# A Fox/RWKV-7 block on one core: q and k stored once per pair of heads, and the order of vector work in the RWKV stage

## The chip, the core and the metric

The kernel runs on one NeuronCore of a Trainium2 chip. The metric is the device time of one execution in microseconds (us). The engines are named as the profile names them: PE (TensorE, matmuls; PEld is its weight load), DVE (VectorE, elementwise work), ACT (ScalarE, activations), POOL (GpSimd), SP (SyncE, which here only issues DMAs; SPq is its queue).

## What is computed

One transformer block over 1,024 tokens of width 1,024, in float32: a norm modulated by a condition c, one wide projection `w_in`, two branches that mix over time, a gate for each branch, an output projection, a second modulated norm, and a convolutional feed-forward net. The two branches matter here. The first is causal attention with forget gates (8 heads of 64); the second is the RWKV-7 recurrence (8 heads of 64):

```python
logits = einsum('bhqd,bhkd->bhqk', q, k) * scale + cum[:, :, q0:q1, None] - cum[:, :, None, :q1]
probs = softmax(where(causal, logits, -inf)); o = einsum('bhqk,bhkd->bhqd', probs, v)

def step(state, inp):
    r_t, w_t, k_t, v_t, a_t, b_t = inp
    sa = einsum('bhvk,bhk->bhv', state, a_t)
    state = state * w_t[..., None, :] + sa[..., None] * b_t[..., None, :] + v_t[..., None] * k_t[..., None, :]
    return state, einsum('bhvk,bhk->bhv', state, r_t)
```

## The kernel before, in words

**Precision.** Most products are made of three passes: each operand is split into a rounded high part (hi, made on ACT) and the rest (lo, made on DVE), and hi·hi, hi·lo and lo·hi are added up in PSUM. One projection tile of 128 columns and 512 tokens is 24 matmuls. The split of a loaded weight tile is `load_w` (L272: hi on L288, lo on L290).

**Stages.** Projections of the low-rank parts and their chain (to about 145 us of the span), the RWKV stage (to about 611 us), attention (to about 820 us), then the branch outputs, `w_o` and the feed-forward net, which the change doesn't touch.

**How work is woven.** PE's instructions run in the order of the program (`manual_schedule`). The program is written by a small planner, `Weave` (L49): chains of dependent work are Python generators that yield a number of nanoseconds; until that much matmul time has been given out, the planner fills PE with steps of queued projections (L105, L117). `weave.now` is the planner's own clock; it counts matmuls only. The chains have ranks: main before pre. The queue of fillers holds q and k of the attention heads (`qk_steps`, L406, eight weight tiles), v (`v_steps`, L963, two) and sixteen gate tiles (`gate_steps`, L343; in attention `late_gate`, L1174, where the bank is named rk_ps). The r, k, v tiles of RWKV go ahead of these. The order of the other engines in the RWKV stage is not the program's: a scheduler with a timeline of its own sets it from readiness and program order, and `add_manual_dep` with NOSYNC puts one instruction of an engine behind another one of the same engine.

**q and k.** For each pair of heads (i % 4) and each half of the tokens `qk_steps` makes qh on ACT (L413) and ql on DVE (L415), both in a ring of two buffers (sp0), and stores them to DRAM tensor `d_st` (L419). `d_st` has four planes for each head: [q hi; q lo], [k hi; k hi], [q hi; forget rows], [k lo; forget rows]. So some parts are stored twice, with two DMAs each of 64 rows: six DMAs of 128 KB for one half. `forget` (L644) stores the four rows of the forget gates for all heads (L684, L685). `load_head` (L1017) loads a head for attention with three DMAs from POOL: stA (planes 0 and 1, 128 rows), stB (planes 2 and 3, 68 rows), vh.

**A unit of RWKV** is one pair of heads and one half of the tokens (eight chunks of 64); there are eight units, k = 0 to 7. `pre` (L720) makes a unit's operands:

- cum, el, en (decays), the norm of kk by a head sum (ssq), then eight elementwise steps on DVE: ar (L760), kr (L761), bk (L762), ar (L764), al (L765, L766), bk (L767), rkb (L771), given out together; then `yield 10500`;
- p, the products of a chunk (L784), masked into E on DVE (L787);
- the inverse of the triangular 32x32 blocks: E's blocks go through DRAM (sm, L795) to the tile M (M32 in the code, L799), then 31 steps of two DVE instructions (L807, L809), back through DRAM (se, L812) to TT (L820);
- q, a product whose copy to QA is L846, and the bonus (bon, L850), made from the head sum bs. The scan of cum (L737) of the next unit is placed behind the bonus.

`main` (L853) continues once `ready` is reached, a time on the planner's clock set at L800 (E's end plus 49,500, 38,500 or 41,000): X on DVE (two transposes, L865), placed behind marks such as the last state (S) and the last E; xi, zi, uw, mz and the chain of states (sp, yp); then y, its mean by a head sum (mu), y minus mean on DVE (L946), the square, its head sum (va), and the end of the norm. A head sum (`head_sums`, L710) makes hi on ACT (L712) and lo on POOL (L715), yields 3,400 and issues two matmuls.

**After the RWKV stage** the first head's loads are given out (L1027), the gate in hand is completed (L1031), and attention begins; its logits (`s_chain`, L1047) wait 10,500 ns of filling gate matmuls.

Of the kernel before, what the change touches and what calls it, by code (L numbers as in the profile page):

```python
# [10 lines left out]
F32R = mybir.dt.float32r  # L11
AF = mybir.ActivationFunctionType
ALU = mybir.AluOpType
# [3 lines left out]
S = 1024  # L17
# [5 lines left out]
CH = 64  # L23
# [12 lines left out]
NOSYNC = mybir.DependencyInfo(mybir.DependencyClass.NoSync, mybir.DependencyReason.DATA)  # L36
# [96 lines left out]
def hybrid_block(ctx: ExitStack, tc: tile.TileContext, a, out):  # L133
    nc = tc.nc
    weave = Weave()
# [23 lines left out]
    dr = ctx.enter_context(tc.tile_pool(name="dr", bufs=1, space=bass.MemoryType.DRAM))  # L159
# [6 lines left out]
    def V(name, i=0, n=1):  # L166
        o, _ = VEC[name]
        return vec[:, o + i : o + i + n]
# [30 lines left out]


    d_gate = dr.tile([16, 128, S], F32, name="d_gate")
    d_st = dr.tile([8, 4, 128, S], F32R, name="d_st")
    d_v = dr.tile([8, 128, 8, 128], F32R, name="d_v")
    d_orw = dr.tile([4, 128, S], F32, name="d_orw")

# [34 lines left out]
            nc.vector.tensor_tensor(dst[:, cs], ps, bb[:, cs], op=ALU.add)  # L240

    marks = {}
    held = []

    def behind(i, x):
# [120 lines left out]
    with ExitStack() as es:  # L366
# [39 lines left out]
        def qk_steps(w, i):  # L406
            sc_ = 0.125 if i < 4 else 1.0
            for hf in range(2):
                cs = slice(hf * NH, hf * NH + NH)
                ps = big(f"qk{i}_{hf}")  # L410
                yield from gemm_steps(ps, w, u, cs)
                hi = gsp.tile([128, NH], F32R, tag="sp0", name=f"qh{i}_{hf}")
                nc.scalar.activation(hi, ps, AF.Copy, scale=sc_)  # L413
                lo = gsp.tile([128, NH], F32R, tag="sp0", name=f"ql{i}_{hf}")
                stt(lo, ps, sc_, f32(hi), op0=ALU.mult, op1=ALU.subtract)  # L415
                h0 = 2 * (i % 4)
                for t, k, r0 in ((hi, 0, 0), (lo, 0, 64), (hi, 2, 0)) if i < 4 else ((hi, 1, 0), (hi, 1, 64), (lo, 3, 0)):
                    for h in range(2):
                        nc.sync.dma_start(f32(d_st[h0 + h, k, r0 : r0 + 64, cs]), f32(t[h * 64 : h * 64 + 64, :]))  # L419

        HS = (slice(0, 64), slice(64, 128))

# [10 lines left out]
        with tc.tile_pool(name="st", bufs=1) as st, tc.tile_pool(name="stp", bufs=2, space=PS) as stp, \  # L433
# [144 lines left out]
        with tc.tile_pool(name="lg", bufs=1, reuse_waits="tile") as lg, \  # L578
# [65 lines left out]
            def forget():  # L644
# [10 lines left out]
                for hf in range(2):  # L655
                    cs = slice(hf * NH, hf * NH + NH)
                    ps = gen(f"f_{hf}")
                    n = 0
                    for x in u:
                        for kt in range(KT):  # L660
# [20 lines left out]
                    nc.scalar.copy(r[:, 3, :], z)  # L681
                    nc.scalar.activation(r[:, 4, :], f32(r[:, 0, :]), AF.Copy, scale=-1.0)
                    nc.scalar.activation(r[:, 5, :], f32(r[:, 1, :]), AF.Copy, scale=-1.0)
                    nc.sync.dma_start(f32(d_st[:, 2, 64:68, cs]), f32(r[:, 0:4, :]))  # L684
                    nc.sync.dma_start(f32(d_st[:, 3, 64:68, cs]), f32(r[:, 2:6, :]))  # L685

            for p in range(4):
                for i in (p, 4 + p):
# [6 lines left out]
        def c3(ap):  # L695
            return ap.rearrange("p (c s) -> p c s", s=CH)
# [23 lines left out]
        def pre(k, p, hf):  # L720

            n = f"{p}_{hf}"
            cs = slice(hf * NH, hf * NH + NH)
# [5 lines left out]
            def chunk_tile(nm, bufs, *dims):  # L729
                return rw.tile([128, *dims], F32, tag=nm, name=f"{nm}{n}", bufs=bufs)  # L730
# [5 lines left out]
            for c0 in (0, 256):  # L736
                i = nc.vector.tensor_tensor_scan(cum[:, c0 : c0 + 256], cst2[:, 128:384], cum[:, c0 : c0 + 256], initial=0.0,  # L737
                                                 op0=ALU.mult, op1=ALU.add)
# [19 lines left out]
                yield 200  # L758
            ar = chunk_tile("ar", 2, 2, NCU, CH)
            stt(ar[:, 0], c3(kr), nkk[:, p : p + 1], el[:, :, 0:CH], op0=ALU.mult, op1=ALU.mult)  # L760
            stt(kr, kr, V("k_k", p), al, op0=ALU.mult, op1=ALU.mult)  # L761
            tt(bk[:, :, 0, :], c3(kr), c3(en), op=ALU.mult)  # L762
            nc.gpsimd.tensor_copy(bk[64:128, :, 2, :], bk[64:128, :, 0, :])
            tt(ar[:, 1], c3(rr), el[:, :, 1:], op=ALU.mult)  # L764
            ts(al, al, V("k_a", p), oka[:, p : p + 1], op0=ALU.mult, op1=ALU.add)  # L765
            tt(al, al, kk, op=ALU.mult)  # L766
            tt(bk[:, :, 1, :], c3(al), c3(en), op=ALU.mult)  # L767
            pcd = chunk_tile("pcd", 3, NCU)
            nc.gpsimd.tensor_copy(pcd, el[:, :, CH])
            rkb = tmp("ksq")  # L770
            stt(rkb, rr, V("r_k", p), al, op0=ALU.mult, op1=ALU.mult)  # L771
            yield 10500


            while (k - 2, 0) not in passed:
# [1 line left out]
            E = chunk_tile("E", 2, NCU, 2, 3, CH)  # L777
# [19 lines left out]
            M32 = chunk_tile("M32", 1, 32, 32)  # L797
            for g in range(4):
                nc.sync.dma_start(M32[g * 32 : g * 32 + 32, :, :], sm.rearrange("h c b s t -> (h c b) s t"))  # L799
            ready = weave.now + (49500 if k == 0 else 38500 if k < 5 else 41000)  # L800
            E32 = chunk_tile("E32", 1, 8, 32)
            nc.gpsimd.dma_start(E32, a["cst"][:, CST["einit"][0] :].rearrange("p (j t) -> p j t", t=32))
            t32 = tmp("t32", 128)
            for s in range(31):
                J, W = s // 4 + 1, 31 - s
                tv = t32[:, 0 : J * W].rearrange("p (j w) -> p j w", w=W)
                tt(tv, E32[:, 0:J, s : s + 1].to_broadcast([128, J, W]),  # L807
                   M32[:, s : s + 1, s + 1 : 32].to_broadcast([128, J, W]), op=ALU.mult)
# [37 lines left out]
            nc.vector.tensor_copy(QA[:, :, 0, :], c3(q))  # L846
# [3 lines left out]
            marks["bonus"] = tt(bon, bp, vv, op=ALU.mult)  # L850
            units[p, hf] = dict(ready=ready, pcd=pcd, ar=ar, E=E, QA=QA, TT=TT, bon=bon, UV=UV)

        def main(k, p, hf):  # L853
# [9 lines left out]
            yield max(0, o["ready"] - weave.now - 2500)  # L863
            for h in range(2):
                i = nc.vector.transpose(X[B0[h], :, :], TT[B0[h], :, 0:32])  # L865
# [80 lines left out]
            stt(y, mu, -1.0 / CH, y, op0=ALU.mult, op1=ALU.add)  # L946
# [68 lines left out]
    heads = {}  # L1015

    def load_head(h):  # L1017
        A = at.tile([128, 2, S], F32R, tag="stA", name=f"stA{h}")
        nc.gpsimd.dma_start(A, d_st[h, 0:2, :, :].rearrange("k r s -> r k s"))
        B = at.tile([128, 2, S], F32R, tag="stB", name=f"stB{h}")  # L1020
        nc.gpsimd.dma_start(B[0:68, :, :], d_st[h, 2:4, 0:68, :].rearrange("k r s -> r k s"))
# [1050 lines left out]
```

## Time and profile before

| what | value |
|---|---|
| median of three runs | 1649.46 us (1647.59 to 1650.44) |
| the profiled execution | 1648.58 us |
| its span, first to last instruction | 1646.8 us |
| mean granted clock of PE | 0.994 |
| busy: PE, DVE, ACT, POOL | 1606.6, 1214.0, 827.6, 159.2 us |

The durations below come from that one profiled execution, and times within it count from the start of its span. A row of a timeline has the start and the duration in us, the engine, the line, the operation, output and inputs, shapes, and in brackets the idle time of the engine ahead of it and what ended this. A row of waits reads: who waited, for whom, us in total, times, the longest. A row of stretches (such as "190.00:192.00") has the length, the busy time and the number of instructions of PE, PEld, DVE, ACT and POOL, then PE's granted clock, the share of the DMA engines and GB/s. Names have no buffer numbers: E32 is E, M32 is M, t32 is t.

### The profile page before, as it was taken

Reading aid. Unit: us, or ns where it says so; the run is one execution under the profiler, and the core shown is the slowest. Engines: PE = TensorE matmul, PEld = TensorE weight load, DVE = VectorE, ACT = ScalarE, POOL = GpSimd, SP = SyncE. Lnnn points to the kernel's source line nnn. Section 1 sums busy time; section 2 is a strip of 40 time slices with the busy share of each in tenths; the row PEclk is TensorE's granted clock in tenths of the full one; section 3 lists DMA queues with packets and bytes.
Section 4 is the critical chain, followed back from the end, with each engine's and each line's share of the span. In section 5 each row is a group of like instructions: output and inputs, shape, how many; then the busy total and the mean of one; then the engine's idle time right before and its main releaser. Section 6 shows DMA issues by size and latency. Waiting matters only on the chain.

```text
span 1646.8 us, 25966 instructions
## 1 busy us (share of the span) xinstructions
PE 1606.6 (98%) x9694; PEld 1339.6 (81%) x9694; DVE 1214.0 (74%) x2345; ACT 827.6 (50%) x1557; POOL 159.2 (10%) x189
## 2 busy tenths in 40 slices
PE   7999999999999999999999999999999999999998
PEld 7777788898978788888888888788888888888886
DVE  4786787878876536888678547887777777886677
ACT  5563345444445656777623235644444444555455
POOL 0011101111111011333132000000000000000000
PEclk9999999999999999999999999999999999999999
DMA  9397645543433336434197420242232232675363
GB/s 338 121 344 229 183 130 139 137 117 94 114 103 98 97 122 163 128 106 118 50 357 264 175 80 26 84 135 96 96 120 98 96 109 96 223 256 160 122 211 109
DMA packets 121646, 240.60 MB, mean 146 GB/s; under 512 B 40048, under 2 KB 48880, under 8 KB 121520
## 3 DMA queue, kind: packets, MB, share of 16 engines
q1 hardware_dynamic: 113040, 220.58, 41.2%
q0 software_dynamic: 8480, 18.37, 4.2%
q8 instruction: 76, 1.25, 0.3%
q14 instruction: 50, 0.41, 0.1%
HBM read 173.35 MB, written 65.54 MB: 145 GB/s over the span
## 4 chain that ended last, share of the span: by engine, by line
PE 58%; DVE 5%; ACT 2%; DMA 2%; issue 1%; SPq 0%; POOL 0%; ACTq 0%; DVEq 0%; POOLq 0%
PE X L141 13%; PE D L141 13%; PE Y L141 6%; PE wo L141 5%; PE br L141 5%; PE W L141 3%; PE rk_ps L141 3%; PE gt L141 3%; PE ov L141 2%; PE lg L141 2%; PE tp L145 1%; DMA vh<-d_v 1%; DVE quads L1075 1%; DVE P L1085 1%; DVE tl L1115 0%
## 5 line engine op out<-in xcount | busy, mean ns | idle before, releaser
L141 PE MATMUL D<-op,op 128*128 128x512 f32 x924 | 209.8, 389 | 0.0
L141 PEld LDWEIGHTS D<-op,op 128*128 128x128 f32 x924 | 173.3, 188 | 36.3 <-DVE op L1295 0.3
L141 PE MATMUL X<-T_m,S 128*128 128x512 f32 x440 | 107.8, 390 | 1.7 <-ACT T_m L1756 1.1
L141 PEld LDWEIGHTS X<-T_m,S 128*128 128x128 f32 x440 | 82.4, 188 | 20.4 <-ACT T_m L1756 2.5
L1294 ACT CAST op<-g 128x512 fp32r<-128x512 f32 x77 | 47.8, 621 | 72.9 <-PE D L141 47.6
L1295 DVE TENSOR_TENSOR op<-g,op 128x512 fp32r<-128x512 f32 x77 | 53.0, 689 | 41.2 <-ACT op L1294 41.2
L1553 DVE SCALAR_TENSOR_TENSOR c<-ab,vec,c 128x512 f32<-128x512 f32 x88 | 65.9, 750 | 18.4 <-ACT c L1556 16.8
L807 DVE TENSOR_TENSOR t<-E,M 128x60 f32<-128x60 f32 (+24 forms) x248 | 55.7, 224 | 26.7 <-DMA M<-sm 20.7
L1519 DVE TENSOR_TENSOR A<-ur,A 128x512 fp32r<-128x512 f32 x64 | 44.0, 689 | 38.7 <-ACT A L1515 38.5
L1519 DVE TENSOR_TENSOR S<-ur,S 128x512 fp32r<-128x512 f32 x66 | 45.5, 691 | 35.2 <-ACT S L1515 35.0
L1515 ACT CAST S<-ur 128x512 fp32r<-128x512 f32 x66 | 41.0, 622 | 55.8 <-DVE ur L1508 30.6
L290 DVE TENSOR_TENSOR lo_in<-raw_in,hi_in 128x512 fp32r<-128x512 f32 x84 | 55.5, 701 | 15.3 <-PE gt L141 4.5
L141 PE MATMUL Y<-T_h,A 128*128 128x512 f32 x264 | 63.7, 390 | 0.3 <-ACT T_h L1756 0.3
L288 ACT CAST hi_in<-raw_in 128x1024 fp32r<-128x1024 f32 x42 | 43.9, 1050 | 40.0 <-PE qk L141 18.6
L141 PE MATMUL Y<-T_h,S 128*128 128x512 f32 x264 | 63.5, 390 | 0.4 <-ACT T_h L1774 0.4
L809 DVE TENSOR_TENSOR E<-E,t 128x60 f32<-128x60 f32 (+24 forms) x248 | 57.6, 232 | 6.3
L1115 DVE TENSOR_TENSOR tl<-tp,th 128x512 fp32r<-128x512 f32 (+1 forms) x80 | 50.0, 631 | 15.3 <-ACT th L1112 15.1
L1515 ACT CAST A<-ur 128x512 fp32r<-128x512 f32 x64 | 39.6, 621 | 42.9 <-PE X L141 31.3
L141 PE MATMUL W<-B_f,A 128*128 128x512 f32 x252 | 60.6, 389 | 0.0
L141 PE MATMUL X<-B_b,A 128*128 128x512 f32 x252 | 60.5, 389 | 0.0
L141 PEld LDWEIGHTS Y<-T_h,S 128*128 128x128 f32 x264 | 49.5, 188 | 11.0 <-ACT T_h L1774 0.8
L141 PEld LDWEIGHTS Y<-T_h,A 128*128 128x128 f32 x264 | 49.5, 188 | 11.0 <-ACT T_h L1756 0.7
(485 smaller groups left out, 4160.6 us busy)
## 6 DMA issues: line engine op xcount, KB each, us to landing
raw_in<-in_w_in SPq DMA_DIRECT2D x50, 512.0 KB, 3.7
wm<-in_w_mod SPq DMA_DIRECT2D x48, 512.0 KB, 7.4
ur<-in_w_up SPq DMA_DIRECT2D x44, 512.0 KB, 4.0
g<-d_g SPq DMA_DIRECT2D x35, 512.0 KB, 4.1
d_g<-gs SPq DMA_DIRECT2D x44, 256.0 KB, 2.1
d_g<-c SPq DMA_DIRECT2D x33, 256.0 KB, 4.5
d_st<-qh SPq DMA_DIRECT2D x64, 128.0 KB, 2.5
stA<-d_st POOLq DMA_DIRECT2D x8, 1024.0 KB, 8.1
```

What stands on the lines that cost most here:

```text
L141: nc.tensor.matmul(o, lhsT, rhs, start=start, stop=stop, skip_group_check=more)
L145: nc.tensor.transpose(o, i, eye)
L288: nc.scalar.copy(hi, raw)
L290: nc.vector.tensor_tensor(lo[:, c : c + NH], raw[:, c : c + NH], f32(hi[:, c : c + NH]), op=ALU.subtract)
L807: tt(tv, E32[:, 0:J, s : s + 1].to_broadcast([128, J, W]), M32[:, s : s + 1, s + 1 : 32].to_broadcast([128, J, W]), op=ALU.mult)
L809: tt(E32[:, 0:J, s + 1 : 32], E32[:, 0:J, s + 1 : 32], tv, op=ALU.add)
L1115: tt(tl[:, 0:w], tp[:, 0:w], f32(th[:, 0:w]), op=ALU.subtract)
L1294: nc.scalar.copy(hi, src)
L1295: tt(lo, src, f32(hi), op=ALU.subtract)
L1515: nc.scalar.copy(hi, src)
L1519: tt(lo, src, f32(hi), op=ALU.subtract)
L1553: stt(c, ab[:, x + hf * NH : x + hf * NH + NH], V("conv_w", 22 * x + i), c, op0=ALU.mult, op1=ALU.add)
```

## The change

Five edits:

1. **q and k once per pair.** `d_st` is replaced by `d_qk` (for each pair of heads: q hi, q lo, k hi, k lo, 128 rows each) and `d_f` (the forget rows for each head). `qk_steps` issues two DMAs of 128 rows for a half. `load_head` puts stA and stB together from five loads on POOL, with vh: stA's rows 0 to 63 (planes 0 and 2), its rows 64 to 127 (planes 1 and 2), stB's rows 0 to 63 (planes 0 and 3), stB's four forget rows, vh.
2. **First inverse step.** In unit 0 the first of the 62 inverse instructions is placed on DVE behind q's copy and behind the bonus.
3. **First main chain later.** The ready time of unit 0 goes from 49,500 to 51,500 ns.
4. **Steps singly.** Seven yields of 800 ns stand between the elementwise steps of every unit, and the yield behind them goes from 10,500 to 4,900.
5. **Last X behind y.** In units 5 to 7 X is placed behind the y minus mean (L946) of the unit before.

```diff
-    d_st = dr.tile([8, 4, 128, S], F32R, name="d_st")
+    d_qk = dr.tile([4, 4, 128, S], F32R, name="d_qk")
+    d_f = dr.tile([8, 2, 4, S], F32R, name="d_f")
...
+    first_step = []
+
+    def after_this(i):
+        for x in first_step:
+            tc.add_manual_dep(x.ins, i.ins.name, NOSYNC)
...
-                h0 = 2 * (i % 4)
-                for t, k, r0 in ((hi, 0, 0), (lo, 0, 64), (hi, 2, 0)) if i < 4 else ((hi, 1, 0), (hi, 1, 64), (lo, 3, 0)):
-                    for h in range(2):
-                        nc.sync.dma_start(f32(d_st[h0 + h, k, r0 : r0 + 64, cs]), f32(t[h * 64 : h * 64 + 64, :]))
+                for t, x in ((hi, 0), (lo, 1)) if i < 4 else ((hi, 2), (lo, 3)):
+                    nc.sync.dma_start(f32(d_qk[i % 4, x, :, cs]), f32(t))
...
-                    nc.sync.dma_start(f32(d_st[:, 2, 64:68, cs]), f32(r[:, 0:4, :]))
-                    nc.sync.dma_start(f32(d_st[:, 3, 64:68, cs]), f32(r[:, 2:6, :]))
+                    nc.sync.dma_start(f32(d_f[:, 0, :, cs]), f32(r[:, 0:4, :]))
+                    nc.sync.dma_start(f32(d_f[:, 1, :, cs]), f32(r[:, 2:6, :]))
...
             stt(ar[:, 0], c3(kr), nkk[:, p : p + 1], el[:, :, 0:CH], op0=ALU.mult, op1=ALU.mult)
+            yield 800
             stt(kr, kr, V("k_k", p), al, op0=ALU.mult, op1=ALU.mult)
+            yield 800
...
-            yield 10500
+            yield 4900
...
-            ready = weave.now + (49500 if k == 0 else 38500 if k < 5 else 41000)
+            ready = weave.now + (51500 if k == 0 else 38500 if k < 5 else 41000)
...
-                tt(tv, E32[:, 0:J, s : s + 1].to_broadcast([128, J, W]),
-                   M32[:, s : s + 1, s + 1 : 32].to_broadcast([128, J, W]), op=ALU.mult)
+                i = tt(tv, E32[:, 0:J, s : s + 1].to_broadcast([128, J, W]),
+                       M32[:, s : s + 1, s + 1 : 32].to_broadcast([128, J, W]), op=ALU.mult)
+                if k == 0 and s == 0:
+                    first_step.append(i)
...
-            nc.vector.tensor_copy(QA[:, :, 0, :], c3(q))
+            after_this(nc.vector.tensor_copy(QA[:, :, 0, :], c3(q)))
...
             marks["bonus"] = tt(bon, bp, vv, op=ALU.mult)
+            after_this(marks["bonus"])
+            first_step.clear()
...
-                for x in ("S", "E", "bank") if k == 0 else ("S", "E", "QA") if k > 4 else ("S", "E"):
+                for x in ("S", "E", "bank") if k == 0 else ("S", "E", "QA", "y") if k > 4 else ("S", "E"):
...
-            stt(y, mu, -1.0 / CH, y, op0=ALU.mult, op1=ALU.add)
+            marks["y"] = stt(y, mu, -1.0 / CH, y, op0=ALU.mult, op1=ALU.add)
...
-        nc.gpsimd.dma_start(A, d_st[h, 0:2, :, :].rearrange("k r s -> r k s"))
+        nc.gpsimd.dma_start(A[0:64, :, :], rows[:, 0:3:2, :])
+        nc.gpsimd.dma_start(A[64:128, :, :], rows[:, 1:3, :])
...
-        nc.gpsimd.dma_start(B[0:68, :, :], d_st[h, 2:4, 0:68, :].rearrange("k r s -> r k s"))
+        nc.gpsimd.dma_start(B[0:64, :, :], rows[:, 0:4:3, :])
+        nc.gpsimd.dma_start(B[64:68, :, :], d_f[h].rearrange("k r s -> r k s"))
```

More of the change, by code (lines that the diff above doesn't have):

```diff
@@ L760, in pre @@
             stt(ar[:, 0], c3(kr), nkk[:, p : p + 1], el[:, :, 0:CH], op0=ALU.mult, op1=ALU.mult)
+            yield 800
             stt(kr, kr, V("k_k", p), al, op0=ALU.mult, op1=ALU.mult)
+            yield 800
             tt(bk[:, :, 0, :], c3(kr), c3(en), op=ALU.mult)
             nc.gpsimd.tensor_copy(bk[64:128, :, 2, :], bk[64:128, :, 0, :])
+            yield 800
             tt(ar[:, 1], c3(rr), el[:, :, 1:], op=ALU.mult)
+            yield 800
             ts(al, al, V("k_a", p), oka[:, p : p + 1], op0=ALU.mult, op1=ALU.add)
+            yield 800
             tt(al, al, kk, op=ALU.mult)
+            yield 800
             tt(bk[:, :, 1, :], c3(al), c3(en), op=ALU.mult)
+            yield 800
             pcd = chunk_tile("pcd", 3, NCU)
@@ L1017, in load_head @@
     def load_head(h):
+        rows = d_qk[h // 2, :, h % 2 * 64 : h % 2 * 64 + 64, :].rearrange("k r s -> r k s")
         A = at.tile([128, 2, S], F32R, tag="stA", name=f"stA{h}")
-        nc.gpsimd.dma_start(A, d_st[h, 0:2, :, :].rearrange("k r s -> r k s"))
+        nc.gpsimd.dma_start(A[0:64, :, :], rows[:, 0:3:2, :])
+        nc.gpsimd.dma_start(A[64:128, :, :], rows[:, 1:3, :])
         B = at.tile([128, 2, S], F32R, tag="stB", name=f"stB{h}")
-        nc.gpsimd.dma_start(B[0:68, :, :], d_st[h, 2:4, 0:68, :].rearrange("k r s -> r k s"))
+        nc.gpsimd.dma_start(B[0:64, :, :], rows[:, 0:4:3, :])
+        nc.gpsimd.dma_start(B[64:68, :, :], d_f[h].rearrange("k r s -> r k s"))
         vh = at.tile([128, 8, 128], F32R, tag="vh", name=f"vh{h}")
```

## The prediction

> **What bounds the kernel now.** I read the page first, then the waits of the matmul engine over the stretch that the change touches (100 to 640 us), then the timelines around each wait.
>
> ```profile
> span 1646.8 us, 25966 instructions
> PE 1606.6 (98%) x9694; PEld 1339.6 (81%) x9694; DVE 1214.0 (74%) x2345; ACT 827.6 (50%) x1557; POOL 159.2 (10%) x189
> ```
>
> The matmul engine (PE) is busy for 1606.6 of 1646.8 us, and the change leaves every matmul as it is. So time can come only from the 40.2 us in which PE stands, and from a lower clock; and time can be lost only by new waits of PE. The waits of PE from 100 to 640 us are few (columns: us in total, times, longest):
>
> ```profile
> PE qk L141 <- DVE ql L415: 1.9, 1, 1.9
> PE v L141 <- DVE vs L978: 1.4, 2, 0.9
> PE rk_ps L141 <- ACT gm L1197: 1.4, 2, 1.2
> PE sp L141 <- ACT S L926: 1.0, 1, 1.0
> PE va L141 <- ACT Zts L712: 1.0, 1, 1.0
> PE va L141 <- POOL Wts L715: 0.9, 1, 0.9
> PE f L141 <- ACT z L619: 0.8, 1, 0.8
> PE zi L141 <- ACT X L875: 0.8, 1, 0.8
> PE p L141 <- DVE bk L767: 0.4, 1, 0.4
> PE mu L141 <- POOL Wtr L715: 0.4, 1, 0.4
> ```
>
> Together they are 10.0 us. So no version of this change can win more than about 10 us and the clock that a stall costs.
>
> **The first inverse step behind q's copy.** VectorE (DVE) around the longest wait:
>
> ```profile
> 182.96 0.19 DVE L807 TENSOR_TENSOR t<-E,M 128x31 f32<-128x31 f32 x1 [6.58 <-DMA M<-sm]
> ...
> 183.30 0.69 DVE L846 COPY QA<-q 128x512 f32<-128x512 f32 x1
> ...
> 186.85 0.68 DVE L850 TENSOR_TENSOR bon<-bs,v 128x512 f32<-128x512 f32 x1
> 187.45 1.26 DVE L737 TENSOR_TENSOR_SCAN cum<-cst,cum 128x256 f32<-128x256 f32 x2
> ...
> 189.94 0.69 DVE L415 SCALAR_TENSOR_TENSOR ql<-qk,qh 128x512 fp32r<-128x512 f32 x1
> ```
>
> The first inverse step of unit 0 stands at the head of DVE's queue for 6.58 us, waiting for M. Behind it stand q's copy, the bonus, the scan of the next unit and the split L415 (ql) that frees the bank PE wants. The inputs of the first two are there early:
>
> ```profile
> 176.49 1.15 PE L141 MATMUL q<-UV,E 64*64 64x64 f32 x32
> ...
> 181.55 0.39 PE L141 MATMUL bs<-al,blk_r 128*128 128x512 f32 x1
> ```
>
> So q's copy can run at 177.7 and the bonus at 182.0, both inside the 6.58 us, and M lands at 182.96 anyway: the first step loses nothing by the new order. Were bs late, the 62 steps behind the first, the store of E, TT, X and unit 0's xi would be late with it, which the later main chain covers up to its 2 us. Of the crowd ahead of ql, 0.60 + 0.60 us go (start to next start, as bon to cum). The scan, 1.18 us from start to start, is held behind the bonus only, so it can go too. PE's stall is 1.87 (the 1.9 above): 0.67 of it stays if the scan doesn't move, none if it does. I take 0.3. The stall also costs clock:
>
> ```profile
> 190.00:192.00 2.00, 1.32 (x5) 1.09 (x6) 1.93 (x7) 1.59 (x3) 0.07 (x1) 0.89 0.12 30
> 192.00:194.00 2.00, 2.00 (x7) 1.51 (x6) 1.79 (x8) 0.00 (x0) 0.00 (x0) 0.50 0.86 190
> 194.00:196.00 2.00, 2.00 (x8) 1.64 (x7) 2.00 (x6) 0.00 (x0) 0.12 (x1) 0.76 0.97 359
> ```
>
> The third number from the right is the granted clock: 2 x (0.11 + 0.50 + 0.24) = 1.7 us of matmul time lost. A gap that is split doesn't do that:
>
> ```profile
> 464.00:467.00 3.00, 1.13 (x4) 0.60 (x4) 0.40 (x1) 2.90 (x6) 1.26 (x1) 1.00 0.66 175
> ```
>
> Here PE stood for 1.02 and then 0.85 us at clock 1.00. So a rest of 0.3 should cost no clock. **Term 1: -(1.6 + 1.7) = -3.3 us**; bounds 0 (the order of DVE comes out with ql late all the same) and -3.6. [...]
>
> **The last X behind y.** Unit 5's X stands ahead of unit 4's y:
>
> ```profile
> 456.60 0.39 PE L141 MATMUL mu<-Wtr,blk_r 128*128 128x512 f32 x1
> ```
>
> ```profile
> 461.70 0.43 DVE L865 STREAM_TRANSPOSE X<-TT 32x256 f32<-32x256 f32 x1 [3.63 <-DMA TT<-se]
> 462.17 0.69 DVE L946 SCALAR_TENSOR_TENSOR y<-mu,y 128x512 f32<-128x512 f32 x1
> ```
>
> Its input mu is done at 457.0, and y starts at 462.17; from y hang the square, its split on ACT and POOL, and the va matmuls that wait 1.02 and 0.85 us. With y first it runs in the 3.63 us of idle, and X is delayed at most by its 0.69, and only if TT lands in that moment. **Term 2: -1.9 us**, bounds 0 and -2.6 (zi's 0.8 behind it might go too).
>
> **The steps given out singly.** In the old order all eight steps of a unit come at one place of the program, and the v evacuations behind them stand in their queue:
>
> ```profile
> 342.08 0.37 ACT L977 CAST vs<-v 128x256 fp32r<-128x256 f32 x1 [2.86 <-PE v L141]
> ```
>
> ```profile
> 345.14 0.42 DVE L978 TENSOR_TENSOR vs<-v,vs 128x256 fp32r<-128x256 f32 x1
> ```
>
> The ACT half of this evacuation ended at 342.45, the DVE half starts 2.7 us later; PE waits for it here and in one more place, 1.4 us together. Seven yields of 800 put later evacuations between the steps (GpSimd's copies of bk and pcd move along, off PE's path): **term 3: -1.4 us**, bounds 0 and -1.4. The steps themselves come up to 5.6 us later of 10.5 (the last yield shrinks from 10,500 to 4,900, so p keeps its place). PE waits for a unit's steps in one unit of eight (p, 0.4), so most units have slack; one evacuation of 0.6 to 0.7 us put ahead costs a unit without slack that much. **Term 4: +0.5 us**, bounds 0 and +1.4 (two units).
>
> **q and k stored once per pair.** Sixty-four of 96 DMA issues leave SyncE (each half had six of 128 KB; now two of 256 KB), and 12 MB written become 8. The buffers of qh and ql come free earlier; one such wait lay in the middle of unit 0's steps, ahead of the p matmul that waited 0.4 us:
>
> ```profile
> 158.59 0.69 DVE L415 SCALAR_TENSOR_TENSOR ql<-qk,qh 128x512 fp32r<-128x512 f32 x1 [1.99 <-DMA d_st<-ql]
> ```
>
> **Term 5: -0.4 us**, bounds 0 and -0.4. On the other side GpSimd issues five loads per head, not three: q/k in three parts of 64 rows (512 KB each), 4 rows of f (32 KB), vh.
>
> ```profile
> stA<-d_st POOLq DMA_DIRECT2D x8, 1024.0 KB, 8.1
> stB<-d_st POOLq DMA_DIRECT2D x8, 544.0 KB, 13.5
> vh<-d_v POOLq DMA_DIRECT2D x8, 512.0 KB, 3.9
> ```
>
> The 68-row stB is the slowest to land, though half of stA. A 512 KB part lies between vh's 3.9 and stB's 13.5 us; I take a value near vh and stA, 4 to 8. Head 0 is the tight one:
>
> ```profile
> 608.90 1.00 POOL L1021 DMA_DIRECT2D stB<-d_st  x1
> ```
>
> ```profile
> stB<-d_st POOLq DMA_DIRECT2D x1, 544.0 KB, 18.9
> ```
>
> ```profile
> 628.24 0.40 PE L141 MATMUL lg<-stB 68*128 68x512 f32 x1
> ```
>
> Its stB landed 18.9 us after 608.90, at 627.8, and the first matmul on it ran at 628.24. At stB's 1.00 us an issue, the third q/k part is issued 1.3 us later than stB was. **Term 6: 0**; its cover is the 10.5 us of gate matmuls given out ahead of the first logits and the rest of the gate before. Bounds 0 and +4.6 (below). The later heads are loaded while most of a head is still computed.
>
> **First main chain later.** 2,000 ns more of filling matmuls before unit 0's X and all that follows. It is no work and no wait: PE does projections in that time, and the two DMAs of a unit's end (gg in, d_orw out) move with it on SyncE's queue. **0**. Some of the shift is swallowed before the last unit, whose start hangs on its own ready time:
>
> ```profile
> 560.53 0.46 PE va L141 x2
> ...
> 567.12 0.62 PE xi L141 x32
> ```
>
> There are 6.1 us from the end of unit 6's va to unit 7's xi, where the code needs 1.3.
>
> **The sum.** -3.3 - 1.9 - 1.4 + 0.5 - 0.4 = -6.5 us. All engines but PE are ordered by a planner that counts with its own durations, and the new waits and edges reorder them. The waits of PE that the change doesn't aim at (sp, zi, mu, f: 3.0 us) show what an order leaves over; I add 0.8 for new ones: **-5.7 us**. The profiled execution took 1648.58 (1646.8 and 1.8 around it) and lies 0.88 under the median, 1649.46: 1642.9 by the one, **1643.8** by the other, which I forecast.
>
> **The rivals.**
>
> 1. A new DVE crowd, or ql late as before: one gap of the kind seen, 1.87 + 1.7, eats 3.6 of the gain: 1647.4. For it: DVE is 74% busy and 62 inverse steps fill its queue. Against: the gap needed a queue blocked for 6.58 us first. Chance 0.14; two such gaps (1651) 0.04.
> 2. The dip of the clock isn't the stall's, and stays: term 1 is -1.6, 1645.5. For it: at 464 to 467 as much idle time, in two pieces, left the clock at 1.00. Against it: the dip begins in the very slice in which the gap of 1.87 ends. Chance 0.05.
> 3. The half loads are as slow as stB was: the last of them lands 18.9 us after an issue 1.3 us later than stB's, at 629.1, and the shift of the chain can leave up to 2 us less of the gate before, so the logits want it at 626.2: 2.9 us of stall and 1.7 of clock, +4.6: 1648.4. [...] Chance 0.04.
> 4. **Slower**: the chain of unit 7 ends past a gate's boundary.
>
> ```profile
> 611.34 1.99 PE L141 MATMUL gt<-u_hi,hi_in 128*128 128x512 f32 x8
> ...
> 616.79 1.98 PE L141 MATMUL rk_ps<-u_hi,hi_in 128*128 128x512 f32 x8
> ```
>
> After the last va the program completes the gate in hand: 24 matmuls, 5.45 us, until 616.79. If va moves back by more than these 5.45 us, a tenth gate (48 matmuls, 10.9 us) is begun and completed there, and attention has six of the sixteen gates to fill its waits instead of seven:
>
> ```profile
> L141 PE MATMUL gt<-u_hi,lo_in 128*128 128x512 f32 x144 | 39.6, 400 | 0.0
> ```
>
> These are nine gates of 16. If attention can't do without the seventh, that is +10.9: 1654.7. Against: the shift is 2.0 us at most and 1.6 of overshoot (seven yields, a matmul of 0.23 each). Chance 0.07.
>
> **Chances and range.** Forecast case 0.60; all waits of the stage gone as well (-10 and less, about 1639) 0.06; rivals 0.14, 0.04, 0.05, 0.04, 0.07. A measurement of this kernel tells some 0.2% (3.3 us) from no change. Faster by more (under 1646.2): 0.60 + 0.06 + 0.05 = 0.71; within: 0.18; slower: 0.11. The range, 1639.0 to 1650.0, takes in rivals 1 to 3 and leaves out some of the best case, rival 4 and the double of rival 1.
>
> **What would show it.** After the change the waits of PE should lack qk <- ql near 190, va <- Zts and Wts near 465, and v <- vs; the granted clock should stay 1.00 from 180 to 200; QA and bon should stand ahead of the first t<-E,M; stB's landing should fall from 13.5 to under 8 us; nine gates should still end before the first rk_ps. Wrong would be: a new wait of over 1.5 us with a slice under clock 0.9, a wait of lg on a load, or gt with 160 instead of 144 matmuls of each kind.

## The result, and the profile after

After the change the median is 1679.69 us (1675.95 to 1680.91, five runs), beside 1647.59 us of the kernel before on the same chip: ratio 1.0189, 95% interval 1.0177 to 1.0200. The change makes the kernel slower by 1.9%. The profiled execution took 1675.95 us, with a span of 1674.2; before it was 1646.8. So there are 27.4 us to account for (this execution was the fastest of the five; by the medians it is 32). The page of the kernel after:

```profile
span 1674.2 us, 25916 instructions
PE 1616.7 (97%) x9694; PEld 1345.3 (80%) x9694; DVE 1218.8 (73%) x2345; ACT 828.0 (49%) x1555; POOL 160.9 (10%) x203
```

PE has the same 9,694 matmuls, is busy 10.1 us longer (the granted clock, 0.991 over the span after 0.994, is at most 5.4 us of it) and stands 57.5 instead of 40.2 us. Where, shows a table of stretches from 100 us on, cut at the first rk_ps (the start of attention) and at the first branch output. Before:

```profile
100.00:616.79 516.79, 507.95 (x4418) 420.08 (x4418) 375.59 (x980) 250.79 (x464) 73.77 (x98) 1.00 0.48 141
616.79:819.88 203.09, 195.34 (x1201) 169.76 (x1200) 155.13 (x302) 148.06 (x337) 55.47 (x68) 1.00 0.40 110
819.88:1646.80 826.92, 816.31 (x3637) 674.20 (x3636) 616.16 (x951) 375.57 (x673) 24.23 (x15) 1.00 0.43 146
```

After:

```profile
100.00:651.52 551.52, 532.74 (x4503) 439.21 (x4502) 384.59 (x987) 259.45 (x479) 78.57 (x104) 0.99 0.42 127
651.52:845.83 194.31, 180.22 (x1105) 156.51 (x1104) 149.16 (x294) 137.79 (x317) 55.16 (x75) 0.98 0.46 104
845.83:1674.20 828.37, 817.63 (x3637) 675.41 (x3636) 617.20 (x951) 375.55 (x673) 22.29 (x15) 0.99 0.43 146
```

The RWKV stage is 34.7 us longer and attention 8.8 us shorter. That is not yet the loss, because gates have moved from the one into the other (groups of the kernel after: count, busy us, mean ns):

```profile
L141 PE MATMUL gt<-u_hi,lo_in 128*128 128x512 f32 x176 | 47.2, 399 | 0.0
L141 PE MATMUL rk_ps<-u_hi,lo_in 128*128 128x512 f32 x80 | 23.7, 406 | 0.0
```

176 matmuls of a kind are eleven gates, not nine; attention has five, not seven. Two gates are 21.8 us of PE (twice the 10.9 of the prediction). Without them the RWKV stage lost 34.7 - 21.8 = 12.9 us. Attention should have become 21.8 shorter and became 8.8 shorter: 13.0 lost. PE stands 14.1 instead of 7.8 us in it, at a granted clock of 0.98. The rest of the kernel lost 1.4.

The order on PE shows why. Before, first product of the third pair's r, k, v, and the first norm (ssq) that needs them:

```profile
295.75 1.09 PE L141 MATMUL ps_rkv<-u_hi,hi_in 128*128 128x512 f32 x4
...
328.29 0.63 PE L141 MATMUL ssq<-kp,blk_r 128*128 128x512 f32 x2
```

After, with the end of the stage:

```profile
292.74 1.11 PE L141 MATMUL v<-hi_v,u_hi 128*128 128x256 f32 x8
...
328.10 0.39 PE L141 MATMUL ps_rkv<-u_hi,hi_in 128*128 128x512 f32 x1
...
358.72 0.63 PE L141 MATMUL ssq<-kp,blk_r 128*128 128x512 f32 x2
...
598.38 0.69 PE L141 MATMUL xi<-X,E 32*32 32x32 f32 x32
642.44 0.39 PE L141 MATMUL va<-Wts,blk_r 128*128 128x512 f32 x1
```

A tile of attention's v has gone ahead of r, k, v of unit 4. Unit 4's norm comes 30 us later. Its xi comes only 10 us later (428.33, before 418.42), so most of this is swallowed; from unit 6 on, whose r, k, v are put on the list when unit 4's operands are done, it is over 30: unit 7's xi comes at 598.38 instead of 567.12. PE fills the longer chain with two more gates.

The code says how. r, k, v of the third pair are put at the head of the queue when `pre` of unit 2 ends. This `pre` waits until `main` of unit 0 has passed a point, and that hangs on unit 0's ready time. The next weight tile is fetched when the last qk tile begins. On the planner's clock the kernel before has the three tiles on the list at 226.1 us and fetches at 228.4. The changed kernel has them at 228.4 and fetches at 227.2, so v's tile, next in the queue, is taken. Writing the program out with other ready times shows two edges. The order above begins between 51,400 and 51,500 ns in the kernel before, and between 51,200 and 51,250 with the other four edits, so 51,500 lies less than 300 ns past it. Another turn comes much earlier, past 49,740 (past 49,510 with the other edits): the second v tile goes ahead of r, k, v of unit 5, and attention loses one or two gates. The margin to the first turn was thus some 250 ns, with the other edits under 50. No run here has that first turn by itself.

The five longest waits of PE after, from 100 us to attention (total, times, longest):

```profile
PE sp L141 <- ACT S L942: 6.1, 3, 3.6
PE xi L141 <- DVE X L881: 4.2, 2, 2.8
PE uw L141 <- ACT TT L898: 2.6, 1, 2.6
PE mz L141 <- DVE Wt L909: 1.3, 1, 1.3
PE gt L141 <- DVE gs L366: 1.0, 1, 1.0
```

None is a wait that the change aims at: those (qk, va, v <- vs, p) are gone. Here is the anatomy of the longest new one:

```profile
394.78 0.69 DVE L864 TENSOR_TENSOR bon<-bs,v 128x512 f32<-128x512 f32 x1
...
396.10 0.68 DVE L742 TENSOR_TENSOR_SCAN cum<-cst,cum 128x256 f32<-128x256 f32 x1
...
396.82 0.63 ACT L747 ACTIVATE el<-cum 128x512 f32<-128x512 f32 x1 [10.52 <-DVE cum L742]
...
398.13 0.31 ACT L942 ACTIVATE S<-sp,pcd 128x64 f32<-128x64 f32 x1
...
398.50 0.43 PE L141 MATMUL sp<-S,Mt 128*128 128x64 f32 x2 [3.60 <-ACT S L942]
```

ACT stands 10.52 us with el at the head of its queue. el waits for the scan, the scan for the bonus, and the bonus comes late in a stretch in which DVE hardly stands (busy for 9.3 of the 10 us from 388 to 398). The state S, on which the next matmul hangs, is queued behind el, and el is not urgent. My reading is that the order on two engines fits another plan of PE than the one that runs. The gap costs clock as well:

```profile
398.00:400.00 2.00, 1.50 (x8) 1.36 (x9) 1.83 (x9) 1.18 (x5) 0.23 (x1) 0.82 0.44 118
400.00:402.00 2.00, 2.00 (x11) 2.00 (x11) 1.79 (x8) 1.30 (x3) 0.00 (x0) 0.50 0.60 186
```

### The profile page after: what moved, and what is told of

Same layout as the page of the kernel before. It is cut to its first block, busy times and chain, and to the rows that moved or that the text cites. A ratio compares the mean times of both kernels' runs of the same rounds, so it can differ in the third digit from the quotient of the medians.

```text
span 1674.2 us, 25916 instructions
## 1 busy us (share of the span) xinstructions
PE 1616.7 (97%) x9694; PEld 1345.3 (80%) x9694; DVE 1218.8 (73%) x2345; ACT 828.0 (49%) x1555; POOL 160.9 (10%) x203
## 4 chain that ended last, share of the span: by engine, by line
PE 60%; DVE 4%; ACT 2%; DMA 1%; issue 1%; SPq 0%; ACTq 0%; DVEq 0%
PE X L141 14%; PE D L141 13%; PE Y L141 7%; PE wo L141 5%; PE br L141 5%; PE gt L141 5%; PE W L141 3%; PE rk_ps L141 3%; PE lg L141 2%; PE ov L141 2%; PE tp L145 1%; DVE P L1104 1%; DVE quads L1094 1%; DVE tl L1134 1%; ACT P L1098 0%
## 5 line engine op out<-in xcount | busy, mean ns | idle before, releaser
L297 DVE TENSOR_TENSOR lo_in<-raw_in,hi_in 128x512 fp32r<-128x512 f32 x88 | 59.3, 714 | 36.7 <-PE gt L141 12.7
L1134 DVE TENSOR_TENSOR tl<-tp,th 128x512 fp32r<-128x512 f32 (+1 forms) x80 | 49.8, 630 | 12.9 <-ACT th L1131 12.7
```

The source lines that it names most:

```text
L297: nc.vector.tensor_tensor(lo[:, c : c + NH], raw[:, c : c + NH], f32(hi[:, c : c + NH]), op=ALU.subtract)
L1134: tt(tl[:, 0:w], tp[:, 0:w], f32(th[:, 0:w]), op=ALU.subtract)
```

## The experiments

**Two theories.** A: the later main chain turned the order of the filling projections round, and the loss is that order and the two gates. B: the other edits crowd DVE, and the order does little. The first runs take the change apart.

**e1: the change without the later chain** (`51500` back to `49500`).

> The changed kernel with unit 0's ready time back at 49,500; the four other edits stay. In program order its fillers then come as before (r, k, v of unit 4 ahead of the first v tile; nine gates ahead of attention, seven in it). Theory A (the later main chain pushes the end of unit 2's operands past the point at which the next weight tile is fetched, so v comes ahead of unit 4's r, k, v, units 4 to 7 start late and two gates leave attention): a ratio to before of 0.996 to 0.999, none of the waits sp <- ACT S of over 2 us, xi <- DVE X. Theory B (the four other edits crowd DVE and the loads; the later chain is harmless): the ratio stays at 1.013 to 1.02.

Measured: 1649.62 beside 1647.04, ratio 1.0018 (1.0010 to 1.0027), span 1648.6, nine gates. So four edits of five cost 3 us and not 32: B falls as the main cause. But their gain isn't there either (A said 0.996 to 0.999); that is the second question, below.

**e2: the later chain alone**, the kernel before with the one constant.

> The kernel before with one number changed: unit 0's ready time 51,500 in place of 49,500. Theory A: v ahead of unit 4's r, k, v, ten gates ahead of attention, ratio 1.008 to 1.017. Theory B: within 0.3% of before.

Measured: 1677.23, ratio 1.0189 (1.0173 to 1.0205), ten gates ahead of attention, where the changed kernel has eleven: the whole loss from one constant.

**e3: the order alone**, without that constant; in the kernel before, `pre` of unit 2 puts r, k, v on the list later:

```diff
                 yield from pre(k, p, hf)
+                if k == 2:
+                    yield 3000
                 if p < 3:
                     weave.first.extend(rkv_items(p + 1, hf))
```

> The kernel before with one line: the chain of operands yields 3,000 ns behind unit 2 before it appends the r, k, v tiles of unit 4. Nothing else moves by itself; the ready time stays. Theory A: the same order of fillers as with the later chain alone, and about its ratio, 1.008 to 1.017. Theory B: within 0.3% of before.

Measured: 1675.78, ratio 1.0178 (1.0164 to 1.0192), ten gates ahead of attention. The order by itself is enough. The yield doesn't make unit 3 late as well: its xi comes at 369.92, before at 370.75. Both e2 and e3 lie a little above A's 1.008 to 1.017.

**e5: all five edits, order held.** The fetch of the next weights waits for r, k, v:

```diff
+            if not self.first and {18: 2, 17: 4, 15: 5}.get(len(self.queue), -1) > self.units:
+                break
...
+                weave.units = k
+                weave.prefetch()
```

> The changed kernel with all five edits, but the fetch of the next weight tile is held where it would flip the order: the first v tile waits until unit 2's operands are done, the second until unit 4's, the second gate until unit 5's. Order of fillers and number of gates then are those of before. Theory A: ratio 0.995 to 1.000 although the chain is later. Theory B: 1.013 to 1.02 as the changed kernel.

Measured: 1654.55, ratio 1.0046 (1.0034 to 1.0059), span 1652.1, nine gates; A had said 0.995 to 1.000. Its stretches (RWKV stage from 100 us, attention):

```profile
100.00:620.50 520.50, 508.78 (x4413) 419.70 (x4412) 375.95 (x979) 250.77 (x463) 74.76 (x100) 1.00 0.42 130
620.50:823.70 203.20, 195.07 (x1202) 169.72 (x1201) 156.18 (x303) 148.17 (x337) 60.47 (x82) 1.00 0.50 113
```

That closes the account of the 27.4 us between the spans: 1.8 for four edits (e1 less before), 3.5 for the delay with the order held (e5 less e1), 22.1 for the order (after less e5). Of the 22.1, attention's two gates are 194.31 + 21.8 - 203.20 = 12.9, and the RWKV stage 31.0 - 21.8 = 9.2. By the medians the three are 2.6, 4.9 and 24.6. A is shown as the main cause: the order alone makes the loss (e3), and holding it takes most of the loss away (e5).

**e4: only the two gates moved**, with everything else as before:

```diff
-    while len(weave.queue) > 12:
+    while len(weave.queue) > 4:
```

> The kernel before, with one number changed: the planner completes gates ahead of attention until four gate tiles are left to it, not until twelve entries are, so that attention has two gates fewer to fill its waits (as the changed kernel has). The RWKV stage, its order and all of the work stay as they are. Theory (attention can't do without the two gates): the start of attention moves by 21.8 us and attention gets shorter by only 9 to 12; some 10 to 13 us slower, 1657 to 1660, ratio 1.006 to 1.008, with more and longer waits of PE or of the stb/o matmuls between 640 and 850. Rival (attention's waits are covered without them and the 13 us that attention lost in the changed kernel are of another kind, such as the new loads): within 0.2 per cent of before.

Measured: 1668.16 beside 1647.23, ratio 1.0125 (1.0107 to 1.0142). Its attention:

```profile
641.50:835.50 194.00, 178.33 (x1106) 154.85 (x1105) 149.56 (x294) 137.90 (x317) 51.23 (x63) 0.99 0.30 88
```

194.0 us, as in the changed kernel (194.3), with the old loads: the missing gates alone make attention's loss. Two gates cost 12.7 us there. In e3, which takes one gate away, attention took 197.7, 5.5 more than 203.1 - 10.9. In e2, with one gate less too, it took 201.5, 9.3 more; there stB of head 0 came too late, which no other trace here shows:

```profile
658.94 0.50 PE L141 MATMUL lg<-stB 68*128 68x512 f32 x1 [3.20 <-DMA stB<-d_st]
```

These 3.2 us and the 1.7 us of clock behind them (granted clock 0.99 over the 201.5 us) leave 4.4 for the gate. The gates are one reserve for two stages: a gate of 10.9 us that is given out early shortens attention by 6.5 us at most. The rest of e4's loss by the profile, 2.9 us, lies ahead of attention, where gates now follow one another with nothing between (gt <- gs, 4.1 us). The profiled execution was the fastest of e4's four; by the median e4 lost 20.9, above the theory's 10 to 13.

**The second question: where is the gain of the four other edits?** They were to win 6.5 us and lost 3 in e1. The next runs do each alone, on the kernel before.

**e6: the first inverse step alone.**

> The kernel before with edit 2 alone (the first inverse step of unit 0 behind q's copy and the bonus). Theory of the prediction's term 1: the wait qk <- ql of 1.87 us and the dip of the clock at 190 to 196 go, 3.3 us faster, ratio 0.998. Rival (DVE has as much to do as before; the wait comes back elsewhere as another wait of 1 to 2.5 us): within 0.2 per cent of before, ratio 0.999 to 1.001, with a new wait of PE on DVE or on ACT behind DVE between 195 and 600.

Measured: 1652.55, ratio 1.0030 (1.0018 to 1.0042). The wait qk <- ql and its dip are gone. In their place DVE, later SP, PE, and two stretches of clock:

```profile
182.61 0.18 DVE L813 TENSOR_TENSOR t<-E,M 128x31 f32<-128x31 f32 x1
182.71 1.27 DVE L743 TENSOR_TENSOR_SCAN cum<-cst,cum 128x256 f32<-128x256 f32 x2
...
184.47 0.18 DVE L817 TENSOR_TENSOR E<-E,t 128x31 f32<-128x31 f32 x1
```

```profile
220.38 2.60 SPq L820 DMA_DIRECT2D se<-E  x4
```

```profile
228.90 0.21 PE L141 MATMUL xi<-X,E 32*32 32x32 f32 x2 [4.14 <-DVE X L875]
```

```profile
230.00:232.00 2.00, 2.00 (x22) 1.65 (x19) 1.69 (x10) 0.73 (x2) 0.00 (x0) 0.50 0.59 131
232.00:234.00 2.00, 2.00 (x6) 1.54 (x5) 1.30 (x6) 0.59 (x1) 0.00 (x0) 0.50 0.01 5
```

The first step runs as early as before, but the scan and a split of weights now come between it and the second (184.47; before, 183.19). At the end of the 62 steps the store of E is issued 2.7 us later (217.67 before), unit 0's X follows 4.7 us later than before (223.63), and xi stands 4.1 us. So the first step did need its place, and the later main chain, which cost 30 us (e2), was meant as the cover for it: in the changed kernel xi of unit 0 doesn't wait.

**e7: X behind y alone.**

> The kernel before with edit 5 alone (X of units 5 to 7 behind the y of the unit before). Theory of the prediction's term 2: the waits va <- Zts and va <- Wts (1.02 and 0.85 us) near 465 go, 1.9 us faster, ratio 0.9989; all up to 400 us as before. Rival (what stands behind X waits in their place, such as zi, or the scheduler orders DVE anew): within 0.1 per cent of before, or slower by up to 2 us.

Measured: 1648.58, ratio 1.0004 (0.9995 to 1.0013): no difference. Both va waits are gone; there is a new one of almost the same length beside their place, with a dip of its own (granted clock 0.50 from 470 to 474):

```profile
468.00 2.51 PE L141 MATMUL ps_rkv<-u_hi,hi_in 128*128 128x512 f32 x8 [1.82 <-DVE gs L359]
```

**e8: the steps singly alone.**

> The kernel before with edit 4 alone (the elementwise steps of a unit given out singly). Theory of the prediction's terms 3 and 4: v <- vs goes (1.4 us) and 0.5 comes back, 0.9 us faster, ratio 0.9995. Rival (this edit, which touches all of the eight units, is what makes the new waits sp <- S, v <- vs, uw and q <- QA that the four edits together show): slower by 2 to 5 us, ratio 1.001 to 1.003.

Measured: 1650.92, ratio 1.0019 (1.0010 to 1.0028). v <- vs, the aim, is still there (1.6, before 1.4); sp <- S went from 1.0 to 2.5.

**e9: q and k once, alone.**

> The kernel before with edit 1 alone (q and k stored once per pair, five loads for a head). Theory of the prediction's terms 5 and 6: 0.4 us faster to no change, ratio 0.9995 to 1.000; no wait of lg on a load; stB lands in under 10 us. Rival (64 DMA issues fewer on SyncE move the planner's other transfers and the engines' orders, as each of the other edits alone did): slower by 1 to 4 us, ratio 1.001 to 1.0025, with a new wait of PE between 150 and 600 and none in attention.

Measured: 1651.03 beside 1646.91, ratio 1.0026 (1.0014 to 1.0038). The aimed wait of p is gone; attention is as before; a new wait stands ahead of it:

```profile
223.34 3.04 PE L141 MATMUL qk<-u_hi,hi_in 128*128 128x512 f32 x7 [2.71 <-DVE v L390]
```

**e10 and e11: the later chain with the order held, with the first step and without it** (the hold of e5).

> The kernel before with edits 2 and 3 (first step behind q's copy, first main chain 2 us later), and with the order of the filling projections held as before (9 gates ahead of attention, 7 in it). Theory (edit 2 makes unit 0's X late by some 4.5 us, and edit 3 is its cover): the wait xi <- X of 4.5 us that edit 2 alone had falls to about 2.5, the dip of the clock behind it goes or gets shorter, and the time is 2 to 4 us under that of edit 2 alone, ratio 0.999 to 1.0015 of before. Rival (the 2 us of delay cost as much as they cover, or new waits come): ratio 1.002 to 1.004, as edit 2 alone.

> The kernel before with edit 3 alone, and with the order of the filling projections held as before. Theory (the 2 us of delay are themselves nearly free, as the prediction had it; all of edit 3's cost is the order and the two gates): within 0.15 per cent of before, ratio 0.999 to 1.0015. Rival (the delay costs by itself, which would explain why all five edits with the order held were 4.9 us over four edits without edit 3): ratio 1.002 to 1.004, with new waits in the RWKV stage.

Measured: e10 1662.02, ratio 1.0090 (1.0076 to 1.0104); e11 1659.91, ratio 1.0079 (1.0065 to 1.0093). xi of unit 0 stands 2.5 us in e10, as expected, but both times lie outside of what either theory said. The delay alone costs 13 us with nine gates and the old order of the projections; from 300 to 400 us PE stands 7.2 us in e11 (1.0 before), in gaps at zi (2.6), q (1.4), v (1.0) and smaller ones. That part of it is the hold itself, which delays one fetch of weights, isn't excluded.

So the split of the loss depends on where one starts. On the kernel before, the 30.2 us of the constant (e2) are 13.0 with the order held and 17.2 for the order; with the four other edits in place they are 4.9 and 24.6. The costs of the edits don't add up: edits 1, 4 and 5, put on top of e10, give e5, which is 7.5 us faster.

**p1 to p4: shifts that aim at nothing.** After these runs the suspicion was that any new order of DVE and ACT costs something. The kernel before with unit 0's ready time at 49,000, 49,300 and 49,700 ns, and at 50,500 with the hold; the projections and gates stay as they were.

> The kernel before with one constant changed: the ready time of unit 0 is 49,000 instead of 49,500 ns; the order of the filling projections and the nine gates stay. The main chain starts 0.5 us earlier, which aims at no wait. Theory (every edit, also one without an aim, makes the scheduler order VectorE and ScalarE anew, and the order of before is an uncommonly good one): 1 to 5 us slower, ratio 1.0005 to 1.003, with waits of PE between 200 and 600 that before hasn't. Rival (small shifts cost nothing; each of the single edits had a cost of its own): within 0.1 per cent of before.

> The kernel before with the ready time of unit 0 at 49,300 instead of 49,500 ns. Theory (new orders of VectorE and ScalarE cost by themselves): 1 to 5 us slower, another sum than with 49,000. Rival (small shifts cost nothing): within 0.1 per cent of before.

> The kernel before with the ready time of unit 0 at 49,700 instead of 49,500 ns: 0.2 us later, order of the filling projections and gates unchanged. Theory (new orders of VectorE and ScalarE cost by themselves): 1 to 5 us slower. Rival (small shifts cost nothing): within 0.1 per cent of before.

> The kernel before with the ready time of unit 0 at 50,500, 1 us later, and the order of the filling projections held as before. With 2 us it was 13.0 us slower. Theory (new orders cost by themselves, with no law in the size of the shift): anything from 1 to 13 us slower. Rival (the delay costs in proportion to its size): some 6 us slower, ratio 1.003 to 1.005, and 0.2 to 0.5 us of delay would be worth 1 to 3.

| ready time of unit 0 | us (before: 1646.75) | ratio, interval |
|---|---|---|
| 49,000 | 1650.05 | 1.0018 (1.0010 to 1.0027) |
| 49,300 | 1651.70 | 1.0024 (1.0013 to 1.0034) |
| 49,700 | 1647.65 | 1.0004 (0.9996 to 1.0013) |
| 50,500, held | 1650.42 | 1.0020 (1.0012 to 1.0029) |

0.2 us earlier costs 0.24%, 0.5 us earlier 0.18%, 1 us later 0.2%, 2 us later (e11) 0.8%. There is no law in the size of the shift. New orders cost up to 5 us by themselves (p3 can't be told from nothing), as much as each of the edits alone (0.04 to 0.30%). This rests on the medians. A single new wait in one profile says less: e4 and e7 run DVE in the order of before up to 305 us, and both stand 1.0 to 1.2 us near 248 us (ps_rkv <- k), where the kernel before doesn't.

**d1 to d3: the four edits in three more orders**, the changed kernel with 49,300, 49,000 and 48,500 ns. If the four edits' gain were real and only covered by a bad order in e1, other orders would show it.

> The changed kernel with the ready time of unit 0 at 49,300 ns: the four other edits and 0.2 us earlier than before; order of the projections and gates as before. Theory (the four edits' gain of some 6 us is real, and each draw of the order costs 0 to 5 us): this draw and its two sisters come out around 3 us under before on the mean, ratios 0.996 to 1.000. Rival (the waits aimed at are simply replaced; the edits are worth nothing): the three lie where the shifts without the edits lie, 1.000 to 1.0025.

> As d1_edits_49300, with 49,000 ns. Theory (the gain is real beside the draw): 0.996 to 1.000. Rival (edits worth nothing): 1.000 to 1.0025.

> As d1_edits_49300, with 48,500 ns. Theory (the gain is real beside the draw): 0.996 to 1.000. Rival (edits worth nothing): 1.000 to 1.0025; with the chain 1 us earlier and the first step late, xi <- X may wait 1 us longer than in e1 (1.9).

Measured, beside 1646.63: 1655.71, 1655.56, 1656.37; ratios 1.0055 (1.0042 to 1.0068), 1.0053 (1.0041 to 1.0066), 1.0057 (1.0043 to 1.0071). The theory of a hidden gain falls, and the three lie above the rival's range too. With e1, four orders of the four edits lie 3 to 10 us over before, where the four shifts without them lie 1 to 5 over. Three of the four have the same waits in common: xi <- X of unit 0, 2.1 to 2.5 us (1.9 in e1), and v <- vs, 2.1 to 2.4 (1.5 in e1). The first of them was to be expected: these kernels have edit 2, which ends the inverse later, and a main chain that starts earlier and doesn't cover it. So d1 to d3 judge edit 2 along with the others. None of the kernels measured is faster than the one before.

## Why the prediction was wrong, step by step

- **"First main chain later: 0" is the step that failed.** The prediction asked what work and which waits the 2,000 ns add, and found none. It didn't ask what else the planner decides by its clock. Two things hung on it: which weight tile is fetched next, and with it how many gates are left for attention. 22.1 of the 27.4 us are this; another 3.5 are the delay with the order held. Without the other edits the delay with the order held is 13.0 (e11, where the hold may have a part), so "no work and no wait" fails there as well.
- **Rival 4 had the sign and the symptom** (more gates ahead of attention), with another cause and another size. It bounded the shift of unit 7's end by 2.0 and 1.6 us; it was 31 (its xi, 567.12 to 598.38). It priced a lost gate at the whole 10.9 us; measured were 5.5 (e3) and 9.3 (e2) for one, and 12.7 for two.
- **Term 1, the gap and its clock,** was read rightly as far as it went: after the change PE doesn't stand from 180 to 200 us, and the clock stays up:

```profile
190.00:192.00 2.00, 2.00 (x11) 1.65 (x10) 2.00 (x6) 1.10 (x2) 0.80 (x1) 1.00 0.18 66
192.00:194.00 2.00, 2.00 (x10) 1.66 (x9) 2.00 (x6) 0.00 (x0) 0.00 (x0) 1.00 0.35 131
```

  But its size came from one execution. Nine other kernels (e2, e3, e4, e7, e11, p1 to p4) run PE, DVE and ACT in the same order up to 220 us; in the one profile of each the gap is 1.20 to 1.84 us, and only e11 has the dip behind it. The term's 1.7 us of clock isn't what this order usually pays.

  Wrong was "the first step loses nothing by the new order". The scan that was to profit went ahead of the second step, and the chain came out 4.7 us late. The prediction named what would then be late (store, TT, X, xi), but tied it to bs.
- **Terms 2 and 5** removed their waits, and as much (e7) or more (e9) came back in other places.
- **Term 3 was wrong**: v <- vs doesn't go with the steps singly (e8, d1 to d3). In the changed kernel it is gone; v's tiles run at another time there, which is the likely reason, not a tested one.
- **Term 4 and the 0.8 for new waits** were far too small. One new order costs up to 5 us here (p1 to p4). Rival 1, a new gap in place of the old, came true for each edit alone; it was the rule, not one case in seven.
- **Term 6, 0,** was right: in the changed kernel no lg waits for a load, and attention takes 203.20 us with five loads for a head (e5), 203.09 with three. But the cover has luck in it: it is what the gate in hand has left, and in e2, with three loads, it ran out by 3.2 us, close to the 2.9 of rival 3. The loads in the kernel after (count, KB each, median us to landing):

```profile
stA<-d_qk POOLq DMA_DIRECT2D x16, 512.0 KB, 6.8
stB<-d_qk POOLq DMA_DIRECT2D x8, 512.0 KB, 9.8
```

  stB fell from 13.5 to 9.8, not under 8. A half of stA lands in 6.8 us where the whole took 8.1, so the two halves don't cost half each; nothing in the changed kernel waits for them.

## What to carry to other kernels

Where a planner gives out the work, a delay that is "no work and no wait" can still move a decision that is taken by comparing times; before costing it at nothing, look for every choice that reads that clock, and write the order out anew. Work that fills waits is a reserve: count what is left of it at the start of each stage that lives on it, and price a lost piece in that stage (here 4.4 to 6.4 of a gate's 10.9 us, more where a load then comes too late). And where a scheduler orders the other engines, shift one constant by some hundred ns first: the spread (here 0 to 0.24%) is the least that an edit has to win, and in a kernel whose constants fit one order, it is nearly all loss. Read the wait that an edit is to win in more than one profile, too.

## What the runs showed of the hardware

**The dips of the clock lasted 3.41 us or two or three times that.** Between 100 and 1,600 us of the kernel before and of the changed one, and between 150 and 640 us of e2, e3, e5, e10, d1, d3, p1, p2 and p4, there are 26 dips, all at a granted clock of 0.50: 22 of 3.41 us, three of 6.83 and one of 10.24. That is 1.7, 3.4 or 5.1 us of clock. It was 5.1 in e3, where PE itself still stood in the first 3.3 us of the dip, and at least 3.4 behind the 4.14 us of standing in e6 (0.50 over the 6.8 us from 229.2 to 236.0). Gaps of like length went both ways. The kernel before lost 1.7 behind a gap of 1.87 us; e8 has the same gap at the same place, 1.82 long, and loses nothing (clock 1.00 from 186 to 194):

```profile
188.40 1.88 PE L141 MATMUL qk<-u_hi,hi_in 128*128 128x512 f32 x7 [1.82 <-DVE ql L415]
```

The 2.55 us at uw in the changed kernel cost no clock (1.00 from 278 to 286), the 2.55 us at uw in e5 cost 1.7 (a dip from 283.48), and the 1.82 of e7 at least 2.2 (0.50 from 469.5 to 474).

The two gaps at uw differ in where they fall. Within a run the dips start at times that lie whole multiples of 3.413 us apart: in e3 at 300.44, 402.84, 440.38, 518.89 and 559.85, which are 30, 11, 23 and 12 of them; in the changed kernel at 399.29, 549.48, 829.37, 839.61 and 1061.48, which are 44, 82, 3 and 65. Here are slices of 3.413 us, counted from the starts of the run's dips, around two gaps, first that of 1.87 in the kernel before, which lies in one slice:

```profile
184.74:188.15 3.41, 3.41 (x16) 2.81 (x15) 3.10 (x13) 0.16 (x1) 0.00 (x0) 1.00 0.80 207
188.15:191.56 3.41, 1.54 (x7) 0.95 (x7) 3.38 (x9) 2.78 (x5) 0.63 (x1) 1.00 0.10 23
191.56:194.97 3.41, 3.41 (x10) 2.63 (x9) 3.17 (x12) 0.06 (x1) 0.00 (x0) 0.50 0.84 228
```

In the changed kernel the edge of a slice cuts the 2.55 us at uw. PE stands for 0.94 us in one slice and 1.61 in the next, and the clock stays:

```profile
276.41:279.83 3.42, 2.47 (x10) 1.71 (x10) 3.42 (x9) 0.00 (x0) 0.00 (x0) 1.00 0.74 271
279.83:283.24 3.41, 1.80 (x28) 1.61 (x30) 2.40 (x11) 3.32 (x7) 0.22 (x1) 1.00 0.22 77
283.24:286.65 3.41, 3.41 (x21) 2.74 (x18) 3.24 (x12) 1.71 (x5) 0.61 (x2) 1.00 0.41 154
```

In e5 the 2.55 us, from 280.91 to 283.46, lie whole in the 3.41 us ahead of the dip.

In the traces of these two kernels, from 100 to 1,600 us, 867 such slices are at full clock. Half clock followed all three in which PE stands for 1.87 us or more, three of the 14 with 1.10 to 1.75, and none of the 850 with less. What decides in the middle, and why some dips last two or three slices, stays open.

The prediction's rule "a gap that is split doesn't do that" fell: in d1 1.26 and 0.82 us, close together and both in one slice, cost 1.7. In the prediction's own row the two gaps leave 0.46 and 1.42 us in two slices, both at clock 1.00.
